# A LoRA linear layer that stores two rows at either end of a chunk by software DMA: one row in their place

## The chip, the cores and the metric

One core of one Trainium2 chip. The metric is the device time of one execution in microseconds (us); the span of a profile (first to last instruction) is about 1.3 us shorter than the time of the same run. The kernels are compared by the ratio of their fast runs, with a 95% interval. A ratio is the mean time of one kernel's fast runs over that of the other's in the same rounds, so it isn't quite the ratio of the medians that are quoted.

## The reference

```python
x_flat = x.reshape(-1, 256)                      # x: 16 x 2048 x 256, float32
y = x_flat @ W                                   # W: 256 x 256
y = y + scale * (((x_flat @ lora_A) * lora_E) @ lora_B)   # rank 16
```

33.6 MB are read and 33.6 MB written. The low-rank part can be folded into W once, so one 256 x 256 product remains for each row.

## The kernel before

The 32,768 rows are cut into four chunks; a chunk has 64 rows for each of the 128 partitions (64 KB of float32 each). Three chunks fit into a ring in SBUF, the on-chip memory. Results overwrite their inputs in the ring and are stored from there. The sync engine issues all big transfers in a fixed order:

```python
ORDER = [
    ("A",),
    ("L", 0, 0, 16), ("L", 0, 16, 40), ("L", 0, 40, 64), ("L", 1, 0, 32), ("L", 1, 32, 64), ("L", 2, 0, 64),
    ("S", 0, 0, 40), ("S", 0, 40, 64),
    ("L", 3, 0, 32), ("L", 3, 32, 64),
    ("S", 1, 0, 64),
    ("S", 2, 2, 62),          # chunk 2 without its first and last two rows
    ("S", 3, 0, 64),
]
SHARED = 2
END_ROWS = 2
SHARES = (slice(108, 113), slice(0, 108), slice(113, P))
```

The rows that chunk 2's store leaves out are stored by GpSimd ("software" DMA), in three DMAs of 5, 108 and 15 partitions:

```python
    def share(engine, p, landed):
        def ends_of(at):
            return at[p].rearrange("p (q b) k -> p q b k", b=END_ROWS)[:, :: ROWS // END_ROWS - 1, :, :]

        engine.dma_start(out=ends_of(y_chunks[SHARED]), in_=ends_of(rows(SHARED, 0, ROWS))).then_inc(landed, 16)
    # ... GpSimd, after its last cast:
        gpsimd.wait_ge(s_done, (SHARED + 1) * ROWS // CG + NY)
        for p in SHARES:
            share(gpsimd, p, shared_stored)
    # ... the sync engine, after its last issue:
        sync.wait_ge(shared_stored, 16 * len(SHARES))
```

Compute (GpSimd casts, PE transposes and multiplies into PSUM, VectorE and ScalarE empty PSUM) isn't touched by the change.

## Time and profile before

| | before |
|---|---|
| median of the first 3 runs | 161.42 us (160.97 to 161.47) |
| span of the profile | 160.1 us |
| DMA: moved, mean rate | 67.41 MB, 421 GB/s |
| PE busy | 60% |
| hardware DMA queue q1, software queue q0 | 97.2% and 0.9% of the 16 DMA engines |

How to read it: of the 40 slices of the page, each digit is a share of busy time in tenths. Compute has long holes, DMA has none until the end. The time is that of 16 DMA engines, each with a sixteenth of the bytes, and the last of the 16 to finish sets the end. The prediction shows the lines.

### The profile page before, as it was taken

To read this page: it belongs to the slowest core of one execution; us is meant where nothing else is said; L and a number is where in the kernel's file an instruction comes from. 1 tells how busy PE (TensorE), PEld (TensorE's weight loads), DVE (VectorE), ACT (ScalarE), POOL (GpSimd) and SP (SyncE) were. 2 spreads that over 40 slices of the span, in tenths; PEclk is the share of its full clock that TensorE was granted. 3 is DMA by queue.
4 is the path that set the end of the run, shared out by engine and by line. 5 is a ranking of instruction groups with operands and counts; after the bars stand their busy time and mean duration, and the time that the engine had idled before them with its cause. 6 is when DMAs were issued, how large, how long until landed. Compare 5 with 4: busy or idle time off the path is not lost.

```text
span 160.1 us, 2042 instructions
## 1 busy us (share of the span) xinstructions
PE 95.3 (60%) x782; PEld 83.3 (52%) x782; DVE 46.1 (29%) x67; ACT 66.3 (41%) x66; POOL 63.3 (40%) x41
## 2 busy tenths in 40 slices
PE   2749999999999910000799999999993000000000
PEld 1235899999999900000699999999992000000000
DVE  0113355555555510000155555555551000000000
ACT  3000577777777730000077777777775000000000
POOL 1044676777767100003676768686850000000000
PEclk9999999999999985555599999999999555555555
DMA  7999999999979997989999999996997998999965
GB/s 270 426 442 436 411 446 434 475 401 401 598 311 524 442 344 328 481 348 442 430 461 393 475 434 401 524 491 295 524 462 308 481 484 354 480 432 390 523 295 248
DMA packets 2449, 67.41 MB, mean 421 GB/s; under 512 B 512, under 2 KB 528, under 8 KB 784
## 3 DMA queue, kind: packets, MB, share of 16 engines
q1 hardware_dynamic: 2016, 66.60, 97.2%
q0 software_dynamic: 224, 0.52, 0.9%
q10 hardware_dynamic: 208, 0.28, 0.5%
q14 instruction: 1, 0.01, 0.0%
HBM read 33.85 MB, written 33.55 MB: 421 GB/s over the span
## 4 chain that ended last, share of the span: by engine, by line
PE 41%; DMA 32%; POOL 2%; ACT 1%; issue 0%; SPq 0%; ACTq 0%; POOLq 0%
DMA out_dram<-ring 27%; PE psum_y L271 26%; PE psum_xt L251 14%; DMA ring<-in_x_dram 5%; POOL stage L194 2%; PE psum_y L297 1%; ACT ring L217 1%; SPq L146 0%; ACTq L217 0%; POOLq L193 0%
## 5 line engine op out<-in xcount | busy, mean ns | idle before, releaser
L217 ACT COPY ring<-psum_y 128x1024 f32 x64 | 64.8, 1013 | 54.3 <-PE psum_y L271 54.3
L194 POOL CAST stage<-ring 128x2048 bf16<-128x2048 f32 x32 | 60.6, 1896 | 52.8 <-DMA out_dram<-ring 22.1
L271 PE MATMUL psum_y<-weff,xt 128*128 128x256 bf16 x512 | 68.5, 278 | 0.0
L240 DVE COPY xt<-psum_xt 128x1024 bf16<-128x1024 bf16 x64 | 44.3, 691 | 62.9 <-PE psum_xt L251 62.9
L251 PE MATMUL psum_xt<-ident,stage 128*128 128x128 f32 x260 | 41.3, 283 | 23.4 <-POOL stage L194 23.4
L271 PEld LDWEIGHTS psum_y<-weff,xt 128*128 128x128 bf16 x512 | 51.3, 100 | 6.0
L251 PEld LDWEIGHTS psum_xt<-ident,stage 128*128 128x128 f32 x260 | 31.6, 146 | 26.3 <-issue 25.2
L283 PE MATMUL psum_y<-ident 128*128 128x512 f32 x4 | 3.8, 1101 | 2.9 <-POOL ident L172 2.9
L283 PEld LDWEIGHTS psum_y<-ident 128*128 128x128 f32 x4 | 1.2, 324 | 3.9 <-POOL ident L172 2.9
L167 POOL DMA_DIRECT2D out_dram<-ring x3 | 2.0, 675 | 1.5 <-PE psum_y L271 1.5
L222 DVE TENSOR_SCALAR stage<-psum_y,e_sb 16x256 f32<-16x256 f32 x1 | 0.5, 472 | 7.2 <-PE psum_y L289 7.2
L211 ACT ACT_TABLE_LOAD x1 | 1.3, 1283 | 2.1 <-SPq L312 2.1
L297 PE MATMUL psum_y<-stage 16*128 16x256 f32 x4 | 2.1, 670 | 0.0
L231 DVE COPY xt<-psum_xt 128x1024 bf16<-128x1024 bf16 x1 | 0.7, 692 | 3.8 <-PE psum_xt L251 3.8
L297 PEld LDWEIGHTS psum_y<-stage 16*128 16x128 f32 x4 | 1.2, 319 | 0.5 <-issue 0.3
L234 DVE TENSOR_TENSOR weff<-stage,psum_y 128x512 bf16<-128x512 f32 x1 | 0.7, 686 | 1.4 <-PE psum_y L297 1.4
L289 PEld LDWEIGHTS psum_y<-ident,a_sb 128*16 128x16 f32 x2 | 0.3, 137 | 1.2 <-issue 1.2
L170 POOL MEMSET ident<- 128x128 f32 x1 | 0.2, 205 | 1.7 <-SPq L312 1.7
L289 PE MATMUL psum_y<-ident,a_sb 128*16 128x128 f32 x2 | 0.6, 421 | 0.0
L172 POOL TENSOR_SCALAR_AFFINE_SELECT ident<-ident 128x128 f32<-128x128 f32 x1 | 0.3, 283 | 0.2 <-POOL ident L170 0.2
L211 ACT COPY one<-ident 128x1 f32<-128x1 f32 x1 | 0.2, 191 | 0.0
L334 POOL MEMSET const-float32-0.0<- 128x1 f32 x1 | 0.1, 93 | 0.2 <-issue 0.2
(3 smaller groups left out, 0.3 us busy)
## 6 DMA issues: line engine op xcount, KB each, us to landing
ring<-in_x_dram SPq DMA_DIRECT2D x4, 4096.0 KB, 24.6
out_dram<-ring SPq DMA_DIRECT2D x1, 7680.0 KB, 37.1
ring<-in_x_dram SPq DMA_DIRECT2D x2, 3072.0 KB, 17.0
out_dram<-ring SPq DMA_DIRECT2D x1, 5120.0 KB, 43.0
out_dram<-ring SPq DMA_DIRECT2D x1, 3072.0 KB, 42.7
ring<-in_x_dram SPq DMA_DIRECT2D x1, 2048.0 KB, 7.9
out_dram<-ring POOLq DMA_DIRECT2D x1, 432.0 KB, 31.3
stage<-in_W_dram ACTq DMA_DIRECT2D x1, 256.0 KB, 2.8
```

Of the source, the lines that this page charges most:

```text
L167: engine.dma_start(out=ends_of(y_chunks[SHARED]), in_=ends_of(rows(SHARED, 0, ROWS))).then_inc(landed, 16)
L194: gpsimd.tensor_copy(out=stage[n % NS][:], in_=rows(c, b, b + CAST)).then_inc(s_stage[n % NS], 1)
L211: scalar.copy(out=one[:], in_=ident[:, :1])
L217: scalar.copy(out=to, in_=psum_y[i % NY][:]).then_inc(s_free[(i + NY) % UNROLL], 1)
L231: vector.tensor_copy(out=xt[0][:], in_=psum_xt[0][:].bitcast(BF16)).then_inc(s_xt[0], 1)
L234: vector.tensor_add(out=weff[:], in0=w_sb, in1=psum_y[1][:, :KT, :]).then_inc(s_free[0], 1)
L240: vector.tensor_copy(out=xt[g % NX][:], in_=psum_xt[g % NT][:].bitcast(BF16)).then_inc(s_xt[g % UNROLL], 1)
L251: ins = tensor.transpose(psum_xt[i % NT][:, b, :], words[:, at * CG + b, :], ident[:])
L271: ins = tensor.matmul(psum_y[i % NY][:, b, :], xt[i % NX][:, b, t::KT], weff[:, t, :], start=(t == 0), stop=(t == KT - 1),)
L283: ins = tensor.matmul(psum_y[1][:, :2, :], ident[:], ident[:, None, :].to_broadcast([P, 4, P]), start=True, stop=True)
L289: ins = tensor.transpose(psum_y[0][:R, t, :P], a_sb[:, t, :], ident[:])
L297: ins = tensor.matmul(psum_y[1][:, t, :], ate[:, t, :], b_sb, start=True, stop=True)
```

## The change

Its likely intent is less software traffic.

```diff
-    ("S", 2, 2, 62),
+    ("S", 2, 1, 63),
     ("S", 3, 0, 64),
 ]
 SHARED = 2
-END_ROWS = 2
+END_ROWS = 1
```

## The prediction

> **What bounds the kernel now.** I read the page's slices first, then its DMA queues and its chain, then a table by stage, then the queue's issues in order of time, and last the single DMA packets and the landings that the trace records.
>
> The page's slices and queues:
>
> ```profile
> PE   2749999999999910000799999999993000000000
> DMA  7999999999979997989999999996997998999965
> GB/s 270 426 442 436 411 446 434 475 401 401 598 311 524 442 344 328 481 348 442 430 461 393 475 434 401 524 491 295 524 462 308 481 484 354 480 432 390 523 295 248
> q1 hardware_dynamic: 2016, 66.60, 97.2%
> q0 software_dynamic: 224, 0.52, 0.9%
> ```
>
> The reader is to see that the matmul row is zero in two long stretches, while the DMA row is at 7 to 9 tenths everywhere but in the last two slices. Nearly all of it is the sync engine's queue (q1). The queue that the change touches (q0, stores issued from GpSimd, the "software" stores) has 0.52 MB and 0.9% of the DMA engines' time. The chain names PE first:
>
> ```profile
> PE 41%; DMA 32%; POOL 2%; ACT 1%; issue 0%; SPq 0%; ACTq 0%; POOLq 0%
> DMA out_dram<-ring 27%; PE psum_y L271 26%; PE psum_xt L251 14%; DMA ring<-in_x_dram 5%; POOL stage L194 2%; PE psum_y L297 1%; ACT ring L217 1%; SPq L146 0%; ACTq L217 0%; POOLq L193 0%
> ```
>
> I don't follow the chain here: it walks back from the last instruction, and nothing but transfers is under way after 123 us. The table by stage settles it:
>
> ```profile
> 103.00:123.00 20.00, 18.57 (x171) 17.03 (x168) 9.77 (x15) 15.26 (x16) 11.62 (x9) 1.00 0.99 429
> 123.00:150.00 27.00, 0.00 (x0) 0.00 (x0) 0.00 (x0) 0.00 (x0) 0.00 (x0) 0.52 1.00 430
> 150.00:160.00 10.00, 0.00 (x0) 0.00 (x0) 0.00 (x0) 0.00 (x0) 0.00 (x0) 0.50 0.77 327
> ```
>
> The last two numbers are DMA share and GB/s. From 123 us to the end at 160.1 us no compute engine has any work, and the 16 DMA engines are full until they run dry. When they were handed that work is in the order of time:
>
> ```profile
> 103.05 20.12 SPq L160 DMA_DIRECT2D out_dram<-ring  x2
> 117.72 2.02 POOL L167 DMA_DIRECT2D out_dram<-ring  x3 [1.50 <-PE psum_y L271]
> ```
>
> The two stores of line 160 are chunk 2 (issued at 103.05) and chunk 3 (122.83, the last instruction). The three software stores go out between 117.7 and 119.7. So the bound is bytes: a hardware packet of 65,536 B takes 2,418 ns (the usual duration among 384 of them), 27.1 GB/s for an engine. Each engine has 1/16 of 67.1 MB, which is 4.194 MB, and 4.194 MB / 27.1 GB/s = 154.8 us. What the trace adds to that is about 1 us before the first byte, 0.85 us per engine for the weights' queue, and stalls. The span ends when the slowest of the 16 engines lands its last piece. Read from the packets, the engines finish their last data between 158.27 and 159.13, except one at 159.70, whose landing is recorded at 160.05. That last engine is the span.
>
> **What the Trainium skill says.** Four places of its page "DMA: Bandwidth & Descriptors" bear on this.
> (1) "Where 436 GB/s comes from": a ceiling of 435 GB/s for 16 engines. The trace agrees: 16 x 27.1 = 434.
> (2) "Queues, rings and completion order": an engine takes turns between queues at packet boundaries. The trace agrees in kind: from 127 us on an engine does one piece of 65,536 B of q1, then one 4,096 B packet of q0, and again. In this trace a packet of q1 is one partition's whole piece.
> (3) "Why a DMA increments its semaphore by 16 and not by 1": the number of engines k is the largest up to 16 that divides the slowest dimension, and software DMAs with k under 16 take k consecutive engines from a cursor that moves on. For 5, 108 and 15 partitions that is k = 5, 12 and 15 with 1, 9 and 1 partitions each: 5 + 12 + 15 = 32, twice round. So four engines get 1 + 1 = 2 partitions ("light") and twelve get 9 + 1 = 10 ("heavy"). The trace agrees: five q0 packets between 123.3 and 124.3, then rounds of twelve.
> (4) "Specifications": runs of 512 B or more are needed for line rate. The new runs have 1,024 B, so no step is expected there; the 1,024 B rows of lora_B took 46 ns and the 2,048 B rows of W 84 ns in this trace, nearly in proportion.
>
> **The change part by part.** The instructions are the same in number and order on every engine. Only sizes move: the software stores carry rows 0 and 63 of each partition of chunk 2 in place of 0, 1, 62, 63, and the hardware store carries rows 1 to 62 in place of 2 to 61. The sync engine's wait before the hardware store rounds up to the same count (191/4 and 190/4 both give 48), so it goes out at the same time. GpSimd still issues three DMAs of two runs for each partition, so its 0.56 to 0.77 us each should stay.
>
> Removed: 128 software packets shrink from 4,096 B (159 ns) to 2,048 B. I take 84 ns for those, from the row of W's 2,048 B packets, so 75 ns less each. For a heavy engine that is 10 x 75 = 0.75 us less, for a light one 2 x 75 = 0.15 us less.
> Added: 128 hardware packets grow from 61,440 B (2,267 ns) to 63,488 B. Halfway to the 2,418 ns of 65,536 B is 2,343, so 76 ns more each, and every engine has 8 of them: 0.60 us more.
> Sum: a heavy engine has 0.15 us less to do, a light one 0.45 us more. Over all engines (12 x -0.15 + 4 x 0.45) / 16 = 0.00 us: the bytes are the same, and only their division moves. All of it lies in the stretch from 123 us on, where DMA is the only work, so what decides is which engine is last.
>
> The last engine, at 159.70, does one 4,096 B packet between its big ones in every round, so it is heavy: it should end at 159.55. The light ones are known by having no small packet between their big ones: I follow four ends, at 158.27, 158.55, 158.69 and 158.94. (Packets carry no engine's number, so I link them by one's end and the next one's start; two of these four could be exchanged with a neighbour.) With 0.45 more they end at 158.72 to 159.39, still before 159.55. So the span should shrink by 0.15 us, from 160.1 to 159.95, and the time from 161.42 to about 161.3.
>
> The point of the unequal shares, as I read it, is balance. Four engines have slow packets: one shows about 2,578 ns in place of 2,418 from 99 us to 121 us, three others up to 2,661 ns between 135 and 149 us. The lighter share gives such engines back 8 x 159 = 1.27 us; after the change it is 8 x 84 = 0.67 us.
>
> **Rivals.**
> A: a light engine becomes the last. Its slow packets differ from run to run, and with half of the compensation gone there is 0.16 us (159.55 against 159.39) between it and the heavy laggard. If it has half a microsecond more bad luck, the end moves up by some 0.3 us: 161.7. For it: the slow packets are in the trace; against it: the margin in this one trace.
> B: software packets disturb the others. If the slow packets of 135 to 149 us (some 0.7 us for each of three engines) came from descriptor traffic of the software stores, and this halves, the light engines gain 0.3 us; but the heavy laggard has none, so the end hardly moves, 161.2 or so. Against it: the first slow engine starts at 99 us, before any software store.
> C: a software packet costs a fixed time whatever its size. Then heavy engines save nothing and pay the 0.60: 162.0. Against it: 46, 84 and 159 ns for 1, 2 and 4 KB.
> D: it is all hidden, and the time stays at 161.42. There is no slack to hide it in, but 0.15 us is less than the spread of the three runs before (160.97 to 161.47), so C apart it may look like this.
>
> **Range and chances.** The runs before have a spread of 0.5 us, 0.3%. My step is -0.15, rival A and C reach +0.3 and +0.6. I say 161.3, from 160.8 to 161.8. A change of 2% is 3.2 us. The largest single sum here is 0.75 us on one engine, so either side needs a thing that I don't see at all.
>
> **What would show it right or wrong.** Right: q0 at 0.26 MB and about 0.5%, q1 at 66.86 MB; 128 q0 packets of 2,048 B at 80 to 92 ns; chunk 2's packets at about 2,343 ns; the issues at 103.05, 117.7 and 122.83 unchanged within 0.3 us; the same engine last, by less than before, and light engines ending nearer to it. Wrong: a light engine last (A), q0 packets at 159 ns (C), slow packets gone and a gain over 0.4 us (B in a stronger form), or a shift in the stages before 103 us, which the change shouldn't touch.

## The result, and the profile after

In the first six runs of each: after 161.6 us median (161.44 to 161.82), before 161.18 (160.97 to 161.47), ratio 1.0025 with an interval of 1.001 to 1.0041. It is "the same" at 2%, but it is slower, by a quarter of a per cent, clear of noise. I had foretold a shade faster.

The same views of the changed kernel. The slices and queues of the page:

```profile
PE   2749999999999920000899999999994000000000
DMA  7999999999969997979999999997997998989975
GB/s 270 426 454 430 418 434 458 459 393 426 606 278 524 475 311 328 491 327 459 399 485 393 475 442 393 524 458 327 524 437 334 494 467 347 535 367 426 510 311 229
q1 hardware_dynamic: 2016, 66.86, 97.6%
...
q0 software_dynamic: 160, 0.26, 0.4%
```

The table by stage (the last two columns are DMA share and GB/s):

```profile
103.00:123.00 20.00, 18.92 (x174) 17.33 (x171) 10.12 (x15) 15.54 (x16) 11.95 (x9) 1.00 1.01 436
123.00:150.00 27.00, 0.00 (x0) 0.00 (x0) 0.00 (x0) 0.06 (x1) 0.00 (x0) 0.53 1.00 432
```

And the issues of the stores in order of time, first the sync engine's, then GpSimd's:

```profile
103.39 20.12 SPq L160 DMA_DIRECT2D out_dram<-ring  x2
...
118.07 2.02 POOL L167 DMA_DIRECT2D out_dram<-ring  x3 [1.50 <-PE psum_y L271]
```

The reader is to see that nothing large moved. q0 has half its bytes, the DMA engines are full to the end, the issues are 0.35 us later (a little over the 0.3 us that the prediction allowed) but into a queue that never runs dry. These views can't tell why the end is later: they are means over 16 engines, and the question is one engine. For that, the single packets of the trace must be read.

A packet's record has a start, a duration, a size and a queue, but no engine. One engine's packets can be linked, as each starts within a few nanoseconds of the last one's end. One engine is easily followed, because it is out of step: from 100 to 121 us its eight packets of chunk 1's store take 2,568 to 2,592 ns in these two profiles, where the other engines' take 2,418. I call it **S** (not the "S" for a store in ORDER). Its last packets in the profile before and after (start in us, ns, bytes, queue; my own listing of the records, with small marker packets left out):

```
before                            after
118.38  2592  65536  q1           118.40  2592  65536  q1
120.98  2341  61440  q1           120.99  2440  63488  q1
123.31   159   4096  q0           123.43    84   2048  q0
...     (7 more of chunk 2)       ...     (7 more of chunk 2)
                                  139.97    84   2048  q0
...     (4 of chunk 3)            ...     (8 of chunk 3)
149.06   159   4096  q0
...     (the last 4 of chunk 3)   ...
159.08  end                       159.57  end
```

S is a light engine: two software packets. It ends 0.49 us later, where its sum of changes is +0.45. In the profile after it is the last of the 16; all others end by 159.12. In the profile before it ended at 159.08, and one heavy engine, at 159.70, was last. One link in the profile before is a choice: at 154.05 two engines go on within 10 ns of one another. I give S the slower packet (2,599 ns), because the packet that is under way during the closing barrier is slow on S in the other ten profiles too; with the other link S would end at 158.88.

### The profile page after: what moved, and what is told of

The parts are those of the page before. It is cut to its first block, busy times and chain, and to the rows that moved or that the text cites. A ratio compares the mean times of both kernels' runs of the same rounds, so it can differ in the third digit from the quotient of the medians.

```text
span 160.1 us, 2042 instructions
## 1 busy us (share of the span) xinstructions
PE 96.4 (60%) x782; PEld 84.1 (53%) x782; DVE 46.1 (29%) x67; ACT 66.3 (41%) x66; POOL 63.2 (39%) x41
## 4 chain that ended last, share of the span: by engine, by line
PE 42%; DMA 31%; POOL 2%; ACT 1%; issue 0%; SPq 0%; ACTq 0%; POOLq 0%
DMA out_dram<-ring 27%; PE psum_y L271 26%; PE psum_xt L251 15%; DMA ring<-in_x_dram 5%; POOL stage L194 2%; PE psum_y L297 1%; ACT ring L217 1%; SPq L146 0%; ACTq L217 0%; POOLq L193 0%
## 5 line engine op out<-in xcount | busy, mean ns | idle before, releaser
L271 PE MATMUL psum_y<-weff,xt 128*128 128x256 bf16 x512 | 69.2, 280 | 0.0
L251 PE MATMUL psum_xt<-ident,stage 128*128 128x128 f32 x260 | 41.9, 285 | 22.6 <-POOL stage L194 22.6
```

What stands on the lines that cost most here:

```text
L251: ins = tensor.transpose(psum_xt[i % NT][:, b, :], words[:, at * CG + b, :], ident[:])
L271: ins = tensor.matmul(psum_y[i % NY][:, b, :], xt[i % NX][:, b, t::KT], weff[:, t, :], start=(t == 0), stop=(t == KT - 1),)
```

## The experiments

Twelve more runs were made, two of them the kernels before and after again. Rivals of the theory "S loses relief" were: software traffic disturbs the other packets; each software packet has a fixed cost; the shorter runs of 1,024 B are slow; the laggard before belongs to the kernel. All results were correct.

### No software stores at all

```diff
-    ("S", 2, 1, 63),
+    ("S", 2, 0, 64),
...
-        for p in SHARES:
-            share(gpsimd, p, shared_stored)
...
-        sync.wait_ge(shared_stored, 16 * len(SHARES))
```

> No software stores at all: chunk 2 goes out whole by the sync engine's queue. Theory (one slow engine, S, which the shares keep light, ends last as soon as its relief shrinks; the relief is what the software rows are for): S ends at 159.09 in the profile of before; it loses two software packets (-0.32 us) and gains 8 x 151 ns (+1.21), so it ends at 159.98 and the time is 0.9 us over before, about 162.0 against 161.1. The other engines end earlier than before (heavy ones 8 x 151 - 10 x 159 = -0.38 us). Rival 1 (software traffic slows the hardware packets, so less of it is better): at or under the time of before. Rival 2 (software packets have a fixed cost, so halving rows wastes it): none of it is paid here, so under the time of before too.

162.04 us (161.8 to 162.05), ratio 1.0054 (1.004 to 1.0067). S ends at 160.17 and is last; the other fifteen end by 159.10. Both rivals that count software traffic fail: with none of it the kernel is slower still. S's slow packets are there too (2,568 to 2,592 ns), so software DMAs don't make S slow.

### The software rows shared evenly: two rows, then one

```diff
-SHARES = (slice(108, 113), slice(0, 108), slice(113, P))
+SHARES = (slice(0, P),)
```

The first with two end rows (here against before), the second with one (the same line changed in the changed kernel).

> Two rows at either end as before, but one software DMA of 128 partitions, which gives 8 partitions to each of the 16 engines: the same software bytes as before without the imbalance. Theory: S has 8 software packets of 4,096 B in place of 2, 6 x 159 ns = +0.95 us: it ends at 160.04, the time is 162.0 to 162.1 against 161.1, like the kernel without software stores. Rival 1 (the amount of software traffic counts): the time of before, 161.1, for the bytes are the same. Rival 2 (fixed cost of a packet): as before or a little under, as there are as many packets and fewer DMAs.

162.10 us (161.88 to 162.14), ratio 1.0064 (1.005 to 1.0077). S has eight packets of 159 ns and ends at 160.01; the others by 158.96.

> The changed kernel's one row at either end, but as one software DMA of 128 partitions, 8 to each engine. Theory: S gets 16 KB of software data in place of 4 KB, in the packets of 4,096 B that the profile of the changed kernel shows 4 x 159 = 0.64 us against 2 x 84 = 0.17 us: +0.47 us on the changed kernel's 159.57, so 160.04, and 162.0 to 162.1, the same as the other two without imbalance though their software bytes are 0, 0.26 and 0.52 MB. Rival 1: between no software stores and two rows in order of the bytes. Rival 2: slower than two rows evenly shared or the same.

162.0 us (161.89 to 162.04), ratio 1.0054 (1.0041 to 1.0068). S has four packets of 160 ns and ends at 160.17; the others by 159.09. With 0, 0.26 and 0.52 MB of software stores evenly shared, the three times lie within 0.1 us of one another. The amount doesn't count here.

### The same shares in another order

```diff
-SHARES = (slice(108, 113), slice(0, 108), slice(113, P))
+SHARES = (slice(0, 108), slice(108, 113), slice(113, P))
```

With two end rows, as before:

> Two rows as before, with the share of 108 partitions issued first and that of 5 second. Sizes, bytes and packets are the same; only which four engines are light moves round, from the engines 1 to 4 after the cursor to the engines 12 to 15. Theory: S is heavy now, 8 x 159 ns = +1.27 us: it ends at 160.36 and the time is 162.3 to 162.4. Rivals 1 and 2: 161.1 as before, as nothing they count has changed. If the slow engine isn't tied to one engine, also 161.1.

162.3 us (162.09 to 162.33), ratio 1.0073 (1.0059 to 1.0087). S has ten packets of 159 ns, ends at 160.46 and is last by 1.2 us. Only the order of the three issues has changed against before, and with it which engines are light, and it costs 1.15 us. This is the strongest single run: which engine gets the rows counts, not how many rows there are.

With one end row:

> The changed kernel with the share of 108 partitions issued first, so that S is heavy: it has 10 partitions of 2,048 B in place of 2, about 0.80 us of packets in place of 0.17. Theory: S ends at 159.57 + 0.63 = 160.2, and the time is 162.0 to 162.2; the same change with two rows cost S 1.27 us and 1.2 us of time, so with one row it should cost half of it on top of the changed kernel. Rivals that count bytes, packets or run lengths: 161.5 as the changed kernel.

162.04 us (161.84 to 162.38), ratio 1.0058 (1.0045 to 1.0071). S has four packets of 160 ns and two of 84, and ends at 160.19, as expected to the tenth.

### Only two engines light

```diff
-SHARES = (slice(108, 113), slice(0, 108), slice(113, P))
+SHARES = (slice(0, 2), slice(2, P))
```

> Two rows at either end, with shares of 2 and 126 partitions: two engines get 1 partition each, fourteen get 9 (126 has 14 as its largest divisor up to 16), so only the first two engines after the cursor are light. S is one of the engines 1 to 4 after the cursor. Theory: if S is engine 1 after the cursor, it stays light with one packet less (158.93) and the others have 9 packets in place of 10 or 2, ending at about 159.0 at most: 160.9 to 161.1, at or just under the time of before (161.15). If S is one of engines 2 to 4, it has 9 packets, +1.11 us: 160.2 and 162.2. Nothing between is expected. Rivals that count bytes or packets: 161.15.

162.11 us (161.97 to 162.16), ratio 1.0062 (1.0048 to 1.0075). S has nine packets and ends at 160.12. So, counted from 0 at the cursor of the prediction's point (3), S isn't engine 0 or 1; it is one of the engines 2 to 4. As expected, there was nothing between the two outcomes.

### Before and after again

> The kernel before, unchanged, for a second profile. In the first one the last engine (159.70) wasn't the slow engine S but a heavy one that lagged from the first load on. Theory: that laggard was chance; in a second profile S, light with two packets of 159 ns, ends at about 159.1 to 159.4, at or near the last, and no other engine ends after 159.5; time 161.0 to 161.2. If the heavy laggard is there again at 159.7, it belongs to the kernel, and the changed kernel's gain on it was real and was hidden by S.

160.84 us, one run of unknown state. S ends at 158.93, all others by 159.05. There is no engine at 159.7: the heavy laggard of the first profile doesn't belong to the kernel.

> The changed kernel again, against before in the same five rounds, for a tighter ratio and a second profile. Theory (the slow engine S loses half of its relief, +0.45 us, and is last again): S ends at 159.4 to 159.6 by itself, all others by 159.2; ratio 1.002 to 1.003, 161.4 to 161.6 against 161.15. If the +0.25% of the first six runs was chance, the ratio is within 0.001 of 1.

161.38 us (161.24 to 161.87) against 161.14 (161.02 to 161.41), ratio 1.0022 (1.0008 to 1.0036). S ends at 159.52 and is last; the others end by 159.07. In both profiles of the changed kernel S is last, by 0.45 us each time.

### Four rows at either end

```diff
-    ("S", 2, 1, 63),
+    ("S", 2, 4, 60),
-END_ROWS = 1
+END_ROWS = 4
```

> Four rows at either end: twice the software bytes of before, the same shares. Theory: hardware packets of chunk 2 shrink by 4,096 B (8 x 151 = -1.21 us for each engine); software packets are 8,192 B for each partition, so a light engine has +0.32 and a heavy one +1.59 us. S: 159.09 - 0.89 = 158.2; a heavy engine: 158.6 to 159.13 + 0.38 = 159.0 to 159.5. A heavy engine is the last now and S among the first; time 161.2 to 161.5, a little over before (161.15), for the opposite reason to the changed kernel. If the time only fell with more software rows, it would be under 161.0 here.

165.13 us (164.67 to 165.29), ratio 1.0253 (1.0239 to 1.0267): expected 161.2 to 161.5, a miss. The page's software queue and one stage of the table, of this kernel:

```profile
q0 software_dynamic: 400, 1.05, 1.7%
```
```profile
159.00:162.40 3.40, 0.00 (x0) 0.00 (x0) 0.00 (x0) 0.00 (x0) 0.00 (x0) 0.50 0.11 43
```

After 159 us there are still 43 GB/s. I had summed durations and forgotten the turns. The 256 software packets have 4,096 B each, so a heavy engine has 20 of them. In the tail an engine mostly does one software packet after each hardware packet, and there are only 16 hardware packets of chunks 2 and 3. 62 software packets start after 158.6 us; the last software landing is at 160.64, after the last hardware landing at 159.55. That has a second price. These are lines of the sync engine's table of waits, first of this kernel, then of the second run of the changed kernel:

```profile
SPq L146 <- DMA out_dram<-ring: 36.2, 1, 36.2
```
```profile
SPq L146 <- DMA out_dram<-ring: 20.7, 1, 20.7
...
SPq L308 <- SPq L308: 13.4, 1, 13.4
```

The wait shown under line 146 is that for the software stores (line 161 of the kernel before); line 308 is the very last wait, for the hardware stores. Usually the first ends long before the second, and the barrier of all engines at the program's end lies hidden between them: 13.4 us of room in this run. With four rows the first wait ends last, at 160.66, the second finds its stores landed, and the barrier's steps run in the open from 160.66 to 162.38. Added up, the span is 162.4, and the usual 1.3 us on top of it would be 163.7; the profiled run took 164.67, and the trace doesn't say where the remaining 0.9 us went.

### The two rows side by side

```diff
-    ("S", 2, 1, 63),
+    ("S", 2, 0, 62),
...
-            return at[p].rearrange("p (q b) k -> p q b k", b=END_ROWS)[:, :: ROWS // END_ROWS - 1, :, :]
+            return at[p][:, ROWS - 2 * END_ROWS :, :]
```

> The changed kernel's bytes and shares, but the two software rows lie together at the end of the partition's 64 rows (rows 62 and 63, one run of 2,048 B) in place of one row of 1,024 B at either end. Theory: the same relief for S, so the same time as the changed kernel, within 0.1 us. Rival (it is the shorter runs of 1,024 B that cost the 0.25%): the time of before, 161.15, or less.

161.95 us (161.73 to 162.15), ratio 1.0049 (1.0036 to 1.0062): neither theory's number. The edit changed more than I meant. The DMA's shape as built became two-dimensional:

```
-L167 DMACopy out_dram<-ring 108x2x256
+L167 DMACopy out_dram<-ring 108x512
```

In the packets, the share of 108 partitions now comes in rounds of 16 engines in place of 12: fifteen engines with 7 partitions and one with 3. S has packets worth nine partitions (three of 159 ns and three of 84) and ends at 160.11; the others by 159.05. The Trainium skill, page "DMA: Bandwidth & Descriptors", section "Why a DMA increments its semaphore by 16 and not by 1", has this: some direct software copies run on 16 engines with partitions/16, rounded up, each. The run agrees: 7 = 108/16 rounded up. So it failed as a test of the run length, and it became another test of who gets the rows, with the outcome that the theory gives for S at nine partitions. As the shares changed too, the time doesn't test the rival of the short runs. The packets do: 4,096 B take 159 to 160 ns with runs of 1,024 B (changed kernel, even shares) as with runs of 2,048 B (before).

### Why is S slow? Two diagnoses

The store of chunk 1, and those queued behind it, are held until all compute is done:

```diff
-                sync.wait_ge(s_done, -(-(c * ROWS + e) // CG) + NY)
+                sync.wait_ge(s_done, (N_GROUPS if c else -(-e // CG)) + NY)
```

> The kernel before with the store of chunk 1 held back until all compute is done (a diagnosis, far slower: 25.2 MB are stored after 122.8 us, 58 us at 434 GB/s, so about 182 us). It asks why S is slow: its 8 packets of the store of chunk 1 take about 2,578 ns in place of 2,418 while compute runs. Theory 1 (it is compute beside a store that slows this one engine): the 8 slow packets are gone when no compute runs, all 16 engines do the chunk at 2,418 ns. Theory 2 (it is the engine, the rows or the addresses of chunk 1): the 8 slow packets of one engine appear again, later.

184.39 us, one run. Stages of this kernel:

```profile
103.00:123.00 20.00, 19.95 (x183) 18.31 (x181) 10.53 (x16) 15.31 (x16) 12.98 (x9) 1.00 0.08 23
...
127.00:150.00 23.00, 0.00 (x0) 0.00 (x0) 0.00 (x0) 0.00 (x0) 0.00 (x0) 0.50 1.04 448
```

Loads are over, DMA idles beside compute at 23 GB/s, and the stores then run with no compute. No engine has a series of slow packets: the first round takes about 2,490 ns on all of them, then 2,422 with two single exceptions, and fifteen of the engines end within 0.13 us of one another. Theory 2 (engine, rows or addresses alone) is out.

The same with the store released at 113.6 us, after the loads and 9 us before the end of compute (56 groups in place of all):

> The kernel before with the store of chunk 1 held until about 112 us: no load is under way any more, compute runs for 10 us still (a diagnosis, slower: about 171 us). With the store held until compute was over the slow packets of S were gone; this separates compute beside a store from a store that follows straight on loads. Theory 1 (compute beside a store): one engine's first 3 or 4 packets of this store take about 2,570 ns, up to about 122 us, then 2,418. Theory 2 (the turn from loads to stores): no series of slow packets on one engine.

176.47 us, expected about 171. Inconclusive. The first packets take about 2,470 ns on all engines; one engine shows 2,546 and then 2,573, but at 119.3 us seven packets take 2,611 to 2,676 together, and slow packets come on many engines until 152 us, long after compute. It is neither theory's picture.

## Why the prediction was right or wrong

The eleven profiles in which S can be followed fit one sum. S ends at a constant plus its work in the tail, counted at the usual durations: its eight hardware packets of chunk 2 (8 x 2,267 ns with two rows left out at either end, 8 x 2,342 with one, 8 x 2,418 with none) and its software packets.

| kernel | S's software packets, us | S's hardware chunk 2, us | S ends | S's end less both | the latest other | median, us |
|---|---|---|---|---|---|---|
| before, two profiles | 0.32 | 18.14 | 159.08, 158.93 | 140.62, 140.47 | 159.70, 159.05 | 161.14 to 161.18 |
| after, two profiles | 0.17 | 18.74 | 159.57, 159.52 | 140.66, 140.61 | 159.12, 159.07 | 161.6, 161.38 |
| even, one row | 0.64 | 18.74 | 160.17 | 140.79 | 159.09 | 162.0 |
| side by side | 0.73 | 18.74 | 160.11 | 140.64 | 159.05 | 161.95 |
| other order, one row | 0.81 | 18.74 | 160.19 | 140.64 | 159.26 | 162.04 |
| none | 0 | 19.34 | 160.17 | 140.83 | 159.10 | 162.04 |
| even, two rows | 1.27 | 18.14 | 160.01 | 140.60 | 158.96 | 162.10 |
| two engines light | 1.43 | 18.14 | 160.12 | 140.55 | 159.21 | 162.11 |
| other order, two rows | 1.59 | 18.14 | 160.46 | 140.73 | 159.24 | 162.3 |

The fifth column stays within 0.36 us while the work varies by 1.3 us, and the time follows S wherever S is last.

**What was right.** The bound (bytes on 16 engines, ended by the slowest), and the step of a light engine: +0.45 us in the sum, 0.49 and 0.59 us for S's end between the two pairs of profiles. The -0.15 us of the heavy engines is a sum of packet times alone: the latest engine other than S ends at 159.05 in the second profile of before and at 159.12 and 159.07 after. Rival A named the outcome, a light engine becomes the last, but not its reason: it spoke of bad luck in slow packets that differ from run to run, and S's delay is the same each time. The time lay within its range, with the wrong sign; that was luck, as the range was wide enough for a step either way.

C is ruled out by the packets (84 ns for 2,048 B, 159 for 4,096), and D by the two intervals, which both exclude 1. B is half right: the slow packets of the three light engines other than S, nine and six of them over 2,500 ns between 137 and 149 us in the two profiles of before, are gone in both profiles after, with no software stores and with even shares (at most one over 2,500 ns besides S's is left). But these three engines aren't last in any of these profiles, so the time gains nothing. It also means that the prediction misread their part of the balance: with even shares of two rows they aren't slow, so their slow packets aren't what the light share is for.

**The step that failed** is "The last engine, at 159.70, does one 4,096 B packet between its big ones in every round, so it is heavy: it should end at 159.55." That engine lagged from the first load on (the last of the 16 landings of the first load came 0.27 us after the fifteenth, and 0.04 in the second profile), in that one profile. In the second profile of before it is absent, and in neither profile of after is any other engine than S later than 159.12. I took one execution's laggard for a property of the kernel. What decided was the engine with a repeated, identical delay, S, whose slow packets I had quoted but whose end I hadn't followed.

With that a second reading fell: "I follow four ends, at 158.27, 158.55, 158.69 and 158.94". S is one of the four light engines, and it ended at 159.08. So the margin between light and heavy engines wasn't 0.16 us in favour of the light ones; without that laggard S was already level with the latest of the heavy ones (158.93 against 159.05). The kernel before is balanced. Any shift of 0.45 us to S had to show, less the 0.1 us between them, and it did: 0.24 and 0.42 us by the medians.

**A smaller miss**, of 0.04 us on a heavy engine and none on S: I expected 128 software packets of 2,048 B. There are 48 of 4,096 B and 32 of 2,048 B, as the software side packs two partitions' rows into one packet. For a heavy engine that is 4 x 159 + 2 x 84 = 0.80 us in place of my 0.84. The Trainium skill's page "DMA: Bandwidth & Descriptors", section "SWDGE vs HWDGE vs iDMA", says that a packet has preferably up to 4,096 B; I hadn't applied it. The trace agrees for q0. A slip of reading besides: the hardware pieces between the software packets have 65,536 B only in chunk 3; from 127 to about 139 us they are chunk 2's, of 61,440 B.

**Is there a better version?** In the second profile of before the sixteen ends lie between 158.22 and 159.05, with a mean of 158.74. A perfect balance could win the difference of the last to the mean, 0.3 us or 0.2%, no more than the runs spread. Four rows at either end fail on turns, and fewer rows or the other shares that ran give S more to do. I ran no further kernel for it; before is the best of those run.

**What stays open.** What makes S slow. It is slow in the same eight packets in every profile but the two diagnoses. Two things in the traces point to instructions being run. The packet that follows the eight, begun near 121 us, loses 38 to 140 ns in the eleven profiles, and broadly more the later compute ends: 38 with the last compute instruction ending at 122.40 us, 74 at 122.72 (before), 140 at 123.96. And one more packet of S is slow in all eleven, by 146 to 193 ns: the one under way while the engines run the closing barrier. The barrier lies anywhere from 123.8 to 156.4 us, the packet moves with it, and no compute engine is busy then.

These are coincidences in time, not a shown cause. With the store held until after compute the series is gone. But the second part of chunk 0's store, from about 74 to 82 us, partly runs beside compute as well, and in the first profile of before its packets of 24,576 B take 912 ns with none over 940. So compute beside a store isn't enough by itself; the run meant to part this from the turn from loads to stores was inconclusive. Every run carries a span and a granted clock, so none tells whether S is slow when nothing is recorded.

## What to carry to other kernels

Where DMA engines are the bound, totals and mean rates don't decide the last half per cent: find the engine that ends last, in more than one profile, and ask whether its delay is there each time before you build a sum on it. A transfer that looks like clutter (three small software stores in 0.9% of the DMA time) may be there for whom it spares, so ask of each engine what a change gives and takes. Moving the light shares to other engines, with everything else equal, is a cheap test of that.

## What the Trainium skill lacked or had wrong

- "DMA: Bandwidth & Descriptors", "Queues, rings and completion order", gives 9 to 17 descriptors as a typical packet between turns, but no bytes; the records don't count descriptors. In these traces a turn of the hardware queue is one partition's whole piece, up to 65,536 B and 2,418 ns, against 4,096 B and 159 ns for the software queue. So software stores beside big hardware ones mostly advance by one packet in about 2.6 us (2,418 + 159 ns): twenty packets for an engine didn't get done within its 16 hardware packets (165.13 us against 161.16).
- The same page, "Why a DMA increments its semaphore by 16 and not by 1", says that some software copies take 16 engines with partitions/16 each, but not which. Here 108x2x256 (rows apart) ran on 12 engines, and 108x512 (rows together) on 16, and the time went from about 161.5 to 161.95 us with it.
- The same page, "Latency and other measured facts", makes software DMA its best guess, not certain, for why some engines are slower. Here one engine's packets took 2,568 to 2,592 ns in place of 2,418, eight in a row, in a program without any software DMA. (The trace doesn't number the engines, so whether it is one that the page names can't be told.)
- I found no page that says what it costs if a program's software store lands last: here the program's closing barrier came into the open, 1.7 us from 160.66 to 162.38.
